# Moving the values' transfers from GpSimd to SP, lending more tiles and re-ordering a hybrid encoder layer's mixer

## The chip, the cores and the metric

The kernel runs on one core of one Trainium2 chip. The metric is device time in microseconds (us): the median of several runs of one launch. One of the executions was taken by the hardware profiler; its page and its trace are what this text reads. The engines are TensorE (PE; its weight loads are listed as PEld), VectorE (DVE), ScalarE (ACT), GpSimd (POOL) and SyncE (SP), which only issues transfers.

## The reference

One layer of an encoder with 512 positions and width 1024, in float32:

```python
x = x + 0.5 * swiglu(rms_norm(x, ffn1_norm), ...)      # d_ff 2752
u = rms_norm(x, mix_norm) @ w_in                        # [fourier 512 | q 8x64 | k 2x64 | v 2x64]
f = real(fft2(fourier, over positions and 128 channels of a group)) ; f = f @ fnet_w[g] + fnet_b[g]
a = softmax(rope(norm(q)) rope(norm(k)).T / 8) v        # 4 query heads to each key head, no mask
x = x + concat([f, a]) @ w_out
x = x + 0.5 * swiglu(rms_norm(x, ffn2_norm), ...)
y = rms_norm(x, final_norm)
```

## The kernel before

Three stages follow one another: feed-forward layer 1, the mixer, feed-forward layer 2. Every float32 operand of a matmul is held as a high part and a rest (suffixes `h` and `l` in the names below), and a product is three matmuls: high by high, high by rest, rest by high (`product`, L176 to L178). So each operand costs a cast and a subtraction (`lows`, L135) on some engine. The change is to the mixer, and to one step at the start of layer 2.

The mixer is written as small operations with names, and the list `ORDER` says in which order they are put out. Every engine takes its own ones in that order and waits where an operand, a tile or a PSUM bank isn't there yet. Lists beside it say which engine takes some of them: `LOWS_POOL` names the rests that GpSimd subtracts instead of VectorE, `HI_DVE` the high parts that VectorE casts instead of ScalarE, `ADDS_DMA` the rotary adds done by an accumulating DMA from GpSimd instead of VectorE, `SUMS_ACT` the broadcasts of the softmax sums done by ScalarE instead of GpSimd.

The names: `wk`, `wq0` to `wq3`, `wv`, `f0` to `f3`, `fw`, `o0` to `o7`, `g0` are weights, with `.r` (load by SP, 512 KB each, `fw` half of it), `.h`, `.l`. `k.0` to `k.7`, `q0.0`, `v.0` and so on are the projections' steps on TensorE, three matmuls of 512 columns each. `.sq`, `.pq`, `.s0`, `.s1` make the heads' norms (square, sums on TensorE, scaling, power on GpSimd); `.sw`, `.sd`, `.rc`, `.rs`, `.ra` the rotary turn (the other half of the pairs by ScalarE, its swap by four transfers of SP, product with the cosine, with the sine, add); `kw`, `kp`, `km` the norm's factor on the keys; `k0.0` to `k1.3` the keys' four parts, of which `k1.1` and `k1.2` are transfers; `q0.ah`, `.al`, `.bh`, `.bl` the queries' parts.

For tile t of the queries (0 to 3), key head b and block c of the keys' positions the scores are `s`tbc: two matmuls on TensorE. Then `m` (scaling and minimum, VectorE), `e` (exponential, ScalarE), `x` (32 by 32 transposition of the probabilities, VectorE), `h` and `l`. `p0` to `p3` multiply the turned probabilities with the values: 128 matmuls each, that use the array in four pieces of 32 rows. `p0` reads the t = 0, 1 and b = 0 ones, `p1` t = 2, 3 and b = 0, `p2` t = 0, 1 and b = 1, `p3` the others; all four read the same tiles `its`, so that the next one's `h` and `l` wait for the one before. The values are needed with their 32-row blocks repeated: tile `vrep`, which `vr0.0` to `vr0.3` (key head 0) and later `vr1.0` to `vr1.3` (key head 1, not before `p1` has read the old ones) fill with four transfers of 64 KB each, in pieces of 512 bytes. The source of `vr0` lies in the tile that `l103` writes. `o00.c` to `o31.a` take `p`'s results out, `z` and `r` divide by the sums and split.

The Fourier branch is `f00` to `f13` (projection for the positions' transform, `.0` and `.1` are twelve matmuls of 256 columns each; `.u`, `.e`, `.h`, `.l` take it out), `map0` and `map1`, `d00` to `d31` (the positions' transform; eight matmuls for d00, d10, d20, d30, six for the others, `.h`, `.l`), and `c0` to `c3` (channels: `.c`, `.s` on TensorE, three matmuls each; `.q`, `.t`, `.h` on ScalarE, `.o`, `.l` on VectorE). At last `y0.0` to `y7.7` are the output projection's steps, with `.x` (residual), `.h`, `.l` (input of layer 2), `.q`, `.a` (square and its sum). Layer 2 opens with two blocks of eight steps; ahead of the second block's first step stands the `column` (sums of the squares over partitions, on TensorE), and ahead of a later one the `row`, that turns the norm's factors.

All of this shares few tiles: two of tag `g` and two of tag `u`, taken in turn, four for the turned probabilities (`sq` and `x`), eight PSUM banks.

## Time and profile before

| | us |
|---|---|
| runs, median of 3 (lowest, highest) | 830.36 (829.91, 830.60) |
| the profiled execution | 829.37 |
| its span, first to last instruction | 827.5 |
| granted clock of TensorE, mean | 0.999 |
| busy: TensorE, VectorE, ScalarE, GpSimd | 818.3, 598.7, 460.4, 131.4 |

Times in a trace count from the start of the span. In a row of a group stand the line of the kernel, the engine, the operation, what it writes and reads, how often, then its busy time in us and the mean of one in ns, and the engine's idle time before it with what ended that. The mixer takes TensorE from about 335 to 488 us.

### The profile page before, as it was taken

How to read it: one execution, taken by the hardware profiler on the slowest of the kernel's cores; microseconds unless marked ns; L12 is line 12 of the kernel's file. 1: busy time of each engine (PE TensorE's matmuls, PEld its weight loads, DVE VectorE, ACT ScalarE, POOL GpSimd, SP SyncE). 2: the span in 40 equal slices, each digit the busy share in tenths (PEclk: the TensorE clock that was granted, in tenths of full speed). 3: DMA queues.
4: the chain of work that ended last, by engine and by line, in shares of the span. 5: the costliest groups of instructions: out<-in, count | busy, mean ns of one | idle time of the engine just before them, and what ended most of it. 6: DMA issues, size and time to landing. Idle time of an engine off the chain costs nothing.

```text
span 827.5 us, 14438 instructions
## 1 busy us (share of the span) xinstructions
PE 818.3 (99%) x5734; PEld 742.0 (90%) x5734; DVE 598.7 (72%) x927; ACT 460.4 (56%) x799; POOL 131.4 (16%) x135
## 2 busy tenths in 40 slices
PE   9999999999999999999999999999999999999997
PEld 6888998899989998888988888899988998899986
DVE  7987884578646857589998778878646884578562
ACT  7764663356434645567897357546623763266452
POOL 0121000000000000248794301200000000000001
PEclk9999999999999999999999999999999999999999
DMA  7787774457374514327350335877464664456122
GB/s 255 190 192 203 185 205 135 115 170 216 92 197 116 159 39 134 128 76 154 123 103 29 102 100 130 223 189 208 119 191 96 197 185 148 122 162 178 45 81 102
DMA packets 51028, 119.85 MB, mean 145 GB/s; under 512 B 5776, under 2 KB 14608, under 8 KB 50832
## 3 DMA queue, kind: packets, MB, share of 16 engines
q1 hardware_dynamic: 38128, 92.57, 33.7%
q0 software_dynamic: 12560, 26.09, 18.5%
q8 instruction: 45, 0.74, 0.4%
q10 hardware_dynamic: 272, 0.26, 0.1%
q14 instruction: 23, 0.19, 0.1%
HBM read 111.83 MB, written 2.10 MB: 138 GB/s over the span
## 4 chain that ended last, share of the span: by engine, by line
PE 93%; DVE 4%; issue 1%; POOL 1%; ACT 0%; DMA 0%; POOLq 0%; SPq 0%; DVEq 0%; ACTq 0%
PE r L453 23%; PE q L453 12%; PE dn L178 9%; PE dn L176 9%; PE dn L177 9%; PE p L453 6%; PE mix L176 3%; PE mix L177 3%; PE mix L178 3%; PE gu L791 3%; PE gu L176 3%; PE gu L177 3%; PE gu L178 3%; PE mix L1286 2%; PE last L1491 1%
## 5 line engine op out<-in xcount | busy, mean ns | idle before, releaser
L453 PE MATMUL r<-rt,ring 128*128 128x256 f32 x1686 | 204.9, 276 | 0.0
L453 PEld LDWEIGHTS r<-rt,ring 128*128 128x128 f32 x1686 | 198.5, 188 | 0.9
L177 PE MATMUL dn<-at,ring 128*128 128x512 f32 x295 | 114.8, 389 | 0.0
L178 PE MATMUL dn<-at,ring 128*128 128x512 f32 x295 | 114.8, 389 | 0.0
L176 PE MATMUL dn<-at,ring 128*128 128x512 f32 x295 | 114.8, 389 | 0.0
L453 PE MATMUL q<-rt,ring 128*128 128x256 f32 x840 | 106.6, 276 | 0.0
L398 ACT CAST ring<-s 128x1024 fp32r<-128x1024 f32 x70 | 73.5, 1050 | 58.1 <-DVE s L418 51.3
L453 PEld LDWEIGHTS q<-rt,ring 128*128 128x128 f32 x840 | 100.4, 188 | 0.0
L605 DVE SCALAR_TENSOR_TENSOR gx<-dn,gx 128x512 f32<-128x512 f32 x61 | 42.1, 691 | 80.4 <-PE dn L178 80.4
L370 POOL DMA_DIRECT2D s<-in_wgu x35 | 30.0, 858 | 424.0 <-DMA s<-in_wgu 186.3
L135 DVE TENSOR_TENSOR ring<-s,ring 128x1024 fp32r<-128x1024 f32 x70 | 85.3, 1218 | 0.6 <-ACT ring L398 0.6
L168 ACT CAST ring<-raw_dn 128x768 fp32r<-128x768 f32 (+2 forms) x48 | 40.8, 853 | 75.5 <-PE dn L177 70.5
L178 PEld LDWEIGHTS dn<-at,ring 128*128 128x128 f32 x295 | 55.4, 188 | 11.5
L177 PEld LDWEIGHTS dn<-at,ring 128*128 128x128 f32 x295 | 55.4, 188 | 11.1
L176 PEld LDWEIGHTS dn<-at,ring 128*128 128x128 f32 x295 | 55.4, 188 | 11.0
L453 PE MATMUL p<-rt,ring 128*128 128x256 f32 x420 | 53.3, 276 | 0.0
L135 DVE TENSOR_TENSOR ring<-raw_dn,ring 128x768 fp32r<-128x768 f32 (+2 forms) x48 | 46.7, 977 | 7.1 <-ACT ring L168 7.0
L453 PEld LDWEIGHTS p<-rt,ring 128*128 128x128 f32 x420 | 50.2, 188 | 0.0
L135 DVE TENSOR_TENSOR ring<-raw_g,ring 128x1024 fp32r<-128x1024 f32 x36 | 43.8, 1216 | 0.0
L135 DVE TENSOR_TENSOR at<-u,at 128x512 fp32r<-128x512 f32 x35 | 24.2, 692 | 20.3 <-ACT at L508 20.2
L496 DVE TENSOR_TENSOR u<-g,u 128x512 f32<-128x512 f32 x35 | 24.0, 686 | 19.8 <-ACT u L493 19.8
L398 ACT CAST ring<-raw_g 128x1024 fp32r<-128x1024 f32 x35 | 36.8, 1051 | 0.0
(332 smaller groups left out, 1548.6 us busy)
## 6 DMA issues: line engine op xcount, KB each, us to landing
raw_g<-in_wgu SPq DMA_DIRECT2D x36, 512.0 KB, 4.0
s<-in_wgu SPq DMA_DIRECT2D x70, 256.0 KB, 4.2
s<-in_wgu POOLq DMA_DIRECT2D x35, 512.0 KB, 5.6
raw_dn<-in_wd SPq DMA_DIRECT2D x44, 384.0 KB, 3.8
raw_u<-in_wgu SPq DMA_DIRECT2D x35, 256.0 KB, 4.1
raw_gu<-in_wgu SPq DMA_DIRECT2D x11, 512.0 KB, 3.6
raw_o<-in_wo SPq DMA_DIRECT2D x8, 512.0 KB, 3.7
raw_dn<-in_wd SPq DMA_DIRECT2D x5, 448.0 KB, 5.3
```

The costliest lines, as they stand in the source:

```text
L135: (by or nc.vector).tensor_tensor(out=lo, in0=src, in1=asf(hi), op=ALU.subtract)
L168: nc.scalar.copy(hi[:, :n, :], raw[:, :n, :])
L176: nc.tensor.matmul(ps, whi, mhi, start=first, stop=False)
L177: nc.tensor.matmul(ps, whi, mlo, start=False, stop=False)
L178: nc.tensor.matmul(ps, wlo, mhi, start=False, stop=last)
L370: nc.gpsimd.dma_start(out=blocks(t), in_=up, accum_op=ALU.add)
L398: nc.scalar.copy(ts[0], src)
L453: nc.tensor.matmul(ps[:, c], a[:, ks], b[:, i, c], start=first and i == 0 and o == 0, stop=i == KH - 1 and o == 2, skip_group_check=not fi ...
L496: nc.vector.tensor_tensor(out=self["u"], in0=self["g"], in1=self["u"], op=ALU.mult)
L605: nc.vector.scalar_tensor_tensor(out=x[d][:, t], in0=ps[:, t], scalar=0.5, in1=x[d][:, t], op0=ALU.mult, op1=ALU.add)
L791: nc.tensor.matmul(pss[c], w[:, k % 2, c], m[k], start=k == 0 and m is hh and w is hi, stop=k == KD - 1 and w is lo,)
L1286: nc.tensor.matmul(sets[st][a][:, : 8 * 32], vrep[rows, j], its[rows, o, :, 32 * j : 32 * j + 32], start=j == 0 and o == 0, stop=j == 15 a ...
```

## The change

The transfers `vr0`, `vr1`, `k1.1` and `k1.2` are issued by SP instead of GpSimd, on the same bytes seen as float32. The tags `g` and `u` get a third tile each (the norms' row tiles, which are idle during the mixer), in three kinds of places: swapped halves, values and Fourier parts share the `g` tiles, rotary products and `p`'s results the `u` tiles; the turned probabilities get a fifth tile. A tile is no longer taken in turn, but borrowed, and given back once the operations named have been put out. Thirteen names come into `LOWS_POOL` and eight leave it, `k` takes the place of `q2` in `ADDS_DMA`, z2 leaves `SUMS_ACT`, `HI_DVE` changes three names for five, `ORDER` is a new list of the same operations, and the row stands ahead of step 7 instead of 6.

```diff
 LOWS_POOL = """
-000 002 010 011 012 013 100 101 103 110 111 113 200 201 202 203 212 213 300 301 302 303 310 311 313 f3 o0 o1 o2 o4
-o5 o6 wq3
+001 002 003 010 011 012 013 100 102 103 110 111 112 113 200 201 202 203 211 212 213 300 301 302 303 312 313 f0 f1 f2
+f3 fw g0 o0 o1 o2 o7 wq2
 """.split()
 ADDS_DMA = """
-q2
+k
 """.split()
 SUMS_ACT = """
-z0 z1 z2 z3
+z0 z1 z3
 """.split()
 LOWS_DMA = """
...
 HI_DVE = """
-300 f0 o3 o4 wq3
+110 203 o3 o4 o6 o7 wq1
 """.split()
...
 ORDERED = {getattr(mybir.EngineType, e) for e in ("PE", "DVE", "Activation", "Pool", "SP")}
 ORDER = """
-wk.r wq0.r wv.r cos wk.h wk.l wq0.h k.0 k.1 k.2 k.3 k.4 wv.h k.5 wq0.l k.6 wq1.r k.7 k.sq q0.0 wq1.h n1.c k.pq q0.1
-wq3.r n1.m wq1.l wq2.r k.sw k.rs n1.p q0.2 q0.3 q0.4 q1.0 q0.5 k.s0 q1.1 wv.l q0.6 k.s1 k.rc q0.7 kw q0.rc k.ra
-wq2.h q1.2 v.0 q0.sw kp v.1 km q1.3 wq2.l q1.4 f0.r q0.sq q0.rs k1.0 q1.5 k0.0 q1.6 q0.ra k0.3 q0.pq q1.7 q0.ah k0.1
-v.2 v.3 q0.s0 q0.al v.4 k0.2 q0.bh q1.sq q0.bl s002 v.5 q0.s1 q1.sw s000 s001 m000 q1.rc q1.pq m002 q2.0 v.6 q1.sd
-v.7 q1.s0 k1.3 q1.rs q2.1 vt k1.1 s003 wq3.h vp e002 q2.2 q1.ra wq3.l m003 e000 x000 vm q1.ah q2.3 q1.al h000 q2.4
-q2.5 f0.h v0.h f1.r q2.6 x002 q2.7 q2.sw q1.s1 q3.0 s103 v0.l f1.h v1.h vr0.0 s102 k1.2 vr0.1 q3.1 m001 l000 q3.2
-m103 q3.3 f0.l q2.rc q2.sq e001 q1.bh q3.4 q3.5 m102 v1.l q3.6 e102 q1.bl f2.r s101 q2.sd e003 x102 x001 f3.r q3.7
-q3.sw q3.sd x003 s100 f2.h q2.rs q3.sq h002 f03.0 vr0.2 h001 e103 f1.l q3.rc m100 f01.0 h003 q2.ra m101 l001 q3.pq
-l003 q3.rs e100 q3.s0 f02.0 h102 q2.ah l002 q2.pq vr0.3 x100 q2.al q2.s0 q2.bh q3.ra f02.1 l102 q2.s1 f00.0 f00.1
-fw.r s203 s202 f2.l q3.s1 q3.ah x103 q3.al f03.1 s200 e101 f3.h f00.u m202 s201 h100 x101 s302 q3.bh z0.r f01.1 m203
-h103 f02.e e202 m200 h101 f3.l m201 e203 s300 x202 m300 f01.u e200 l100 f02.h l103 o1.r e201 z0.w fw.h f03.e x203
-o2.r q3.bl l101 f03.h f11.0 f02.l s303 f11.1 e300 f11.u m302 x200 p0 x300 e302 h200 f03.l s301 pos fw.l h300 f10.0
-q2.bl s112 h202 h203 f10.1 m301 o00.c m303 l202 x302 e303 m112 e301 l203 l200 o01.c x201 f10.u h302 o00.a f12.0
-o01.a s113 x301 f12.1 l300 h201 f13.0 x303 m113 e112 s110 h303 l302 f12.e x112 s013 h301 s011 s012 l201 f13.1 l303
-m110 m012 l301 m011 o2.h e113 e110 map1 f13.e m013 e012 x012 x110 map0 o2.l map1.h x113 map1.l o1.h o1.l f12.h f13.h
-map0.h e011 z1.r map0.l p1 f12.l z0.p f13.l e013 d00 o10.c o11.c r0.m d01 h112 vr1.1 o5.r d01.h s111 o10.a d00.h d11
-h012 o11.a vr1.2 l112 d10 d00.l d11.h d01.l l012 x013 m111 z1.w h110 c0.s d11.l s213 h113 l110 c0.c c0.q h013 m213
-e111 c0.t z1.p l013 d10.h d21 r1.m x111 d10.l l113 s010 d21.h m010 e213 d20 d31 c1.s h111 d21.l c1.c e010 d20.h c1.t
-c0.o c0.h d31.h l111 x010 d20.l x011 s212 h010 o0.r d30 m212 c1.q c0.l s313 c1.o c2.s h011 e212 s312 d30.h r1.h
-d31.l m312 vr1.0 vr1.3 m313 y2.0 c1.h c2.c c2.q x212 s311 c2.t d30.l e312 e313 c2.o l011 c3.s l010 x213 c3.c c1.l
-c3.q m311 s310 o0.h c3.t p2 x312 r0.h y2.1 e311 s210 c2.h c3.o c3.h m310 e310 y1.0 r0.l h212 y1.1 h312 c2.l s211
-z2.r c3.l x313 m210 o0.l o20.c h213 l212 l312 h313 l213 x311 m211 x310 e210 y2.2 h311 y1.2 y0.0 y0.1 e211 o20.a x211
-l313 h310 y0.2 x210 o21.c z2.w o21.a h210 l210 h211 y0.3 y2.3 l211 l311 r1.l y0.4 z3.r z2.p l310 o3.r z3.w y1.3 r2.m
-p3 y1.4 z3.p r2.h o30.c o31.c y1.5 r2.l y2.4 y2.5 y1.6 o30.a y0.5 o31.a r3.m y2.6 r3.h r3.l y2.7 o3.h y1.7 o5.h y0.6
-o3.l y0.7 o4.r y0.x y3.0 o5.l y3.1 y0.h y3.2 o4.h y1.x y3.3 o6.r y3.4 y0.q o4.l g0.r y3.5 y3.6 y5.0 y5.1 y0.l y4.0
-y3.7 y1.q y4.1 y4.2 y5.2 y5.3 y4.3 y2.x o7.r y5.4 o6.h y1.h y5.5 y3.x o6.l y6.0 y4.4 y3.q y4.5 y4.6 y3.a y2.h y5.6
-y6.1 y6.2 y5.7 y3.h y4.7 y1.a y2.l y5.x y3.l o7.h y6.3 y6.4 y6.5 o7.l y6.6 y7.0 y6.7 y7.1 y2.q y4.x y2.a y1.l y7.2
-y6.x y4.q y4.a g0.h y6.h y4.h y7.3 y7.4 y5.q y5.h g0.l y4.l y7.5 y7.6 y6.q y7.7 y5.a y6.l y6.a y7.x y5.l y7.h y7.q
-y7.l y7.a
+wk.r wq0.r wv.r cos wk.h wk.l wq0.h k.0 k.1 k.2 k.3 k.4 wv.h k.5 wq0.l k.6 wq1.r k.7 k.sq q0.0 wq1.h n1.c wq2.r
+wq1.l n1.m q0.1 k.pq f1.r k.sw q0.2 n1.p q0.3 k.rc q1.0 q0.4 q0.5 q0.6 q0.7 q1.1 k.s0 k.rs k.ra k.s1 q1.2 q1.3 q0.rc
+kw wv.l wq2.h q1.4 q1.5 v.0 kp q0.sw q0.rs v.1 q1.6 q1.7 v.2 km q1.sw k0.0 v.3 q0.sq q0.ra wq2.l v.4 k0.3 v.5 k0.1
+v.6 q0.ah k1.0 q0.bh q0.al k1.3 wq3.r q0.pq v.7 q1.sd q1.rc k0.2 q0.s0 q1.rs vt f0.r q0.s1 q2.0 s003 q1.ra q1.sq
+s000 wq3.h q0.bl m000 q2.1 wq3.l q1.ah s002 f0.h e000 q2.2 s001 m001 q2.3 f0.l x000 vp q2.4 q2.5 vm q2.6 h000 l000
+v0.h f2.r m002 k1.1 f3.r q2.7 e001 q2.sw q3.0 q1.pq q3.1 e002 f1.h q3.2 q2.rc q2.sq q1.al m003 q3.3 x001 q2.sd q3.4
+q3.5 q3.6 q1.s0 f1.l q3.7 q1.s1 q3.sw f2.h s102 e003 x002 v0.l v1.h q2.pq s100 q2.rs q2.ra f2.l s103 q3.rc q2.s0
+f01.0 m100 m102 k1.2 q3.sq q3.sd q2.s1 f01.1 q2.ah x003 s101 e102 e100 q2.al h001 h003 v1.l q3.pq q2.bh f03.0 vr0.0
+q3.rs s202 f01.u s203 h002 m103 vr0.3 q3.s0 s200 x100 m101 q3.ra x102 e101 h102 f03.1 m203 l001 x101 q3.s1 h100 l003
+s013 l100 q3.ah f02.0 m013 e103 l002 m200 h101 m202 x103 e203 f00.0 fw.r l101 vr0.2 f00.1 e013 q2.bl q3.al f3.h pos
+e202 f02.1 f03.e vr0.1 h103 s302 l102 l103 f00.u x203 f3.l s303 f11.0 m303 e200 f02.e x202 m302 f03.h x200 q3.bh
+e303 p0 x303 f03.l x013 q1.bh e302 h202 s301 q3.bl o00.c h303 h203 z0.r s201 h200 o01.c m301 e301 fw.h q1.bl f10.0
+o00.a l200 f10.1 m201 e201 f11.1 o01.a s110 l203 s010 s012 l303 x302 z0.w h302 o2.r x201 m010 l302 m110 f11.u m012
+s113 e010 s300 f12.0 f13.0 s011 o1.r x301 f10.u h201 m300 m113 l202 e110 e300 x300 h301 l201 o2.h m011 f13.1 z0.p
+fw.l e113 z1.r l301 x010 s112 h300 f13.e z1.w l300 x113 e012 r0.m map1 x110 e011 f12.1 f12.e x012 m112 map0 f02.h p1
+map1.h map0.h f02.l o2.l o1.h map0.l f12.h e112 f13.h map1.l s111 f12.l vr1.2 f13.l o10.c h110 m111 vr1.0 h013 d00
+o11.c o10.a e111 h113 d11 h012 d01 s312 o11.a l110 x111 d01.h l013 h010 m312 l113 z1.p d01.l x011 d00.h vr1.1 l012
+l010 e312 d00.l d31 r1.m d11.h d10 x112 d10.h s313 h111 d20 m313 c0.c d11.l d10.l l111 x312 c0.s d30 z2.r s213 h112
+d20.h vr1.3 c1.c c0.q c0.t h011 e313 d21 c1.s d21.h c0.o m213 d30.h c1.t o0.r d20.l d21.l d30.l s212 l112 m212 c1.q
+c1.o d31.h e213 l011 o1.l d31.l e212 c2.s s211 c2.c z2.w o0.h c2.q c2.t s311 p2 x212 m211 r0.h c3.s m311 c1.h o5.r
+e211 c0.h c2.o c2.h x313 c3.c o0.l x211 c0.l e311 s310 h313 l313 s210 c1.l c2.l h312 c3.q c3.t y1.0 h212 y1.1 l312
+y1.2 m310 c3.o e310 y2.0 x213 o20.c y2.1 x311 y0.0 l212 c3.h m210 o21.c x310 h211 e210 c3.l y2.2 y2.3 z2.p l211 o3.r
+y0.1 y0.2 z3.r o20.a x210 y1.3 h310 h213 h210 h311 o21.a l310 l213 r1.h l210 l311 r0.l z3.w r2.m y0.3 r2.h p3 r2.l
+y1.4 r1.l z3.p y1.5 o30.c y1.6 y2.4 o30.a o31.c o31.a r3.m y0.4 r3.h r3.l y2.5 y0.5 y2.6 y2.7 o3.h y1.7 y0.6 o3.l
+o4.r y0.7 o5.h y1.x y2.x y3.0 y3.1 y3.2 o6.r y3.3 y1.q o4.h y3.4 o4.l o5.l y3.5 y4.0 y5.0 y5.1 y0.x y3.6 y3.7 o6.h
+y4.1 y4.2 y0.q o6.l y3.x y5.2 y5.3 y5.4 y2.q y5.5 o7.r y1.a y5.6 y6.0 y5.7 y2.h y1.h y4.3 y1.l y4.4 y6.1 y6.2 y0.h
+y2.a y4.5 y4.6 o7.h y6.3 y4.7 o7.l y6.4 y5.x y3.q y6.5 y7.0 y2.l y3.a y3.h y7.1 g0.r y4.x y6.6 y7.2 y5.h y6.7 y4.h
+y3.l g0.h y7.3 y7.4 y5.l y6.x y5.q y7.5 y5.a y6.h y4.q g0.l y6.q y7.6 y7.7 y0.l y6.l y6.a y7.x y7.h y4.l y7.q y7.l
+y4.a y7.a
 """
...
             @op(f"{name}.sw")
             def _():
-                swaps[name] = sw = tp.tile([P, S], F32, tag="g", name=f"sw_{name}")
+                swaps[name] = sw = borrow(lent_g, f"{name}.ra")
                 if by_dma:
...
             @op(f"{name}.rc")
             def _():
-                rots[name] = r = tp.tile([P, S], F32, tag="u", name=f"rot_{name}")
+                users = ("k0.0", "k0.1", "k0.2", "k0.3", "k1.0", "k1.3") if name == "k" else (f"{name}.al", f"{name}.bl")
+                rots[name] = r = borrow(lent_u, *users)
                 if by_dma:
...
                 if v:
-                    op("k1.1")(lambda own=own, oth=oth, h1=h1, h2=h2: nc.gpsimd.dma_start(out=h1[oth], in_=h2[own]))
-                    op("k1.2")(lambda own=own, oth=oth, h1=h1, h2=h2: nc.gpsimd.dma_start(out=h2[oth], in_=h1[own]))
+                    op("k1.1")(lambda own=own, oth=oth, h1=h1, h2=h2: nc.sync.dma_start(out=asf(h1[oth]), in_=asf(h2[own])))
+                    op("k1.2")(lambda own=own, oth=oth, h1=h1, h2=h2: nc.sync.dma_start(out=asf(h2[oth]), in_=asf(h1[own])))
                     op("k1.3")(lambda own=own, h1=h1, h2=h2: lows(h2[own], rots["k"][own], h1[own]))
...
         @op("vt")
         def _():
-            rots["v"] = tp.tile([P, S], F32, tag="g", name="vt")
+            rots["v"] = borrow(lent_g, "vp")
             nc.scalar.copy(rots["v"], banks["v"])
...
             def spread(a):
...
                     src, dst = slice(32 * i, 32 * i + 32), slice(32 * a, 32 * a + 32)
-                    nc.gpsimd.dma_start(
-                        out=vrep[dst].rearrange("p (c i) e -> p c i e", i=4)[:, :, i],
-                        in_=stage[v][src].rearrange("p c o e -> p c (o e)"),
+                    nc.sync.dma_start(
+                        out=asf(vrep[dst].rearrange("p (c i) e -> p c i e", i=4)[:, :, i]),
+                        in_=asf(stage[v][src].rearrange("p c o e -> p c (o e)")),
                     )
...
             @op(f"f{h}{c}.e")
             def _():
-                fes[h, c] = e = tp.tile([P, 2, 256], F32, tag="g", name=f"fe{h}{c}")
+                fes[h, c] = e = borrow(lent_g, f"f{h}{c}.l").rearrange("p (a b) -> p a b", a=2)
                 for o, how in ((0, ALU.add), (1, ALU.subtract)):
...
             @op(f"c{g}.t")
             def _():
-                fos[g, 1] = o = tp.tile([P, S], F32, tag="g", name=f"fo{g}")
+                fos[g, 1] = o = borrow(lent_g, f"c{g}.l")
                 nc.scalar.activation(
...
             @op(f"x{n}")
             def _():
-                pool, how = (tp, {"tag": "sq"}) if len(turned) % 2 else (mt, {"tag": "x", "bufs": 2})
-                turned[n] = pool.tile([P, S], F32, name=f"x{n}", **how)
+                turned[n] = borrow(lent_x, f"h{n}", f"l{n}")
                 nc.vector.transpose(turned[n], probs[n])
...
             def copied(t):
                 if st not in pair:
-                    pair[st] = tp.tile([P, S], F32, tag="u", name=f"oo{st}")
+                    pair[st] = borrow(lent_u, f"r{st}.l")
                 for a in range(4):
...
         zall = [mp.tile([P, 4, 2], F32, name=f"za{t}") for t in range(4)]
+        def blanks(pool, tag, n):
+            return [pool.tile([P, S], F32, tag=tag, bufs=n, name=f"{tag}{i}") for i in range(n)]
+
+        lent_g = [*blanks(tp, "g", 2), n1.rb]
+        lent_u = [*blanks(tp, "u", 2), n2.rb]
+        lent_x = [*blanks(tp, "sq", 2), *blanks(mt, "x", 2), tp.tile([P, S], F32, tag="acc", name="acc_x")]
+        loans = []
+
+        def borrow(pool, *users):
+            t = pool.pop(0)
+            loans.append((set(users), pool, t))
+            return t
+
         scale = HD**-0.5
...
                 ops.pop(name)()
+                for users, pool, t in loans:
+                    users.discard(name)
+                    if not users:
+                        pool.append(t)
+                loans[:] = [loan for loan in loans if loan[0]]
         assert not ops, list(ops)
...
             prepare(2 * NF)
-        return [[gate(0, {}), gate(1, {0: column, 6: row})]]
+        return [[gate(0, {}), gate(1, {0: column, 7: row})]]
```

## The prediction

> **What bounds the kernel now.** I read the page first, then the busy time in stretches of 20 us through the mixer, then TensorE's waits and its timeline at the places they name.
>
> ```profile
> PE 818.3 (99%) x5734; PEld 742.0 (90%) x5734; DVE 598.7 (72%) x927; ACT 460.4 (56%) x799; POOL 131.4 (16%) x135
> PE 93%; DVE 4%; issue 1%; POOL 1%; ACT 0%; DMA 0%; POOLq 0%; SPq 0%; DVEq 0%; ACTq 0%
> ```
>
> TensorE is busy 818.3 of 827.5 us, and 93% of the chain that ended last is its own. The change leaves every matmul in place, so it can only win what TensorE idles, and it can lose without such a limit. The stretches show where the mixer is tight (columns: TensorE, weight loads, VectorE, ScalarE, GpSimd, clock, DMA share, GB/s):
>
> ```profile
> 360.00:380.00 20.00, 20.00 (x111) 17.26 (x109) 17.68 (x34) 13.67 (x28) 13.13 (x17) 1.00 0.73 157
> 380.00:400.00 20.00, 19.26 (x233) 18.21 (x237) 19.84 (x42) 14.83 (x34) 16.21 (x16) 1.00 0.58 147
> 400.00:420.00 20.00, 20.00 (x261) 18.45 (x254) 19.74 (x50) 17.59 (x49) 17.36 (x15) 1.00 0.33 99
> 420.00:440.00 20.00, 18.43 (x223) 16.07 (x222) 19.95 (x51) 18.78 (x49) 17.52 (x20) 1.00 0.41 68
> ```
>
> From 380 to 440 VectorE is busy 59.5 of 60 us. It has no slack left exactly where TensorE idles, and the granted clock is 1.00, so no clock explains it. TensorE's waits in the mixer name VectorE both times:
>
> ```profile
> PE mix L177 <- DVE ring L135: 1.4, 1, 1.4
> PE mix L1246 <- DVE fe L1135: 0.7, 1, 0.7
> ```
>
> A matmul's busy time covers the next one's issue, so a wait is read better from start to start. The timeline of TensorE at the three places:
>
> ```profile
> 391.55 0.28 PE L1115 MATMUL mix<-ring 128*128 128x256 f32 x1
> 391.66 0.28 PE L1116 MATMUL mix<-ring 128*128 128x256 f32 x1
> 392.68 0.50 PE L1246 MATMUL mix<-ks,qa 128*128 128x512 f32 x1 [0.74 <-DVE fe L1135]
> ...
> 430.16 0.40 PE L1247 MATMUL mix<-ks,qb 128*128 128x512 f32 x1
> 430.39 0.39 PE L176 MATMUL mix<-eh,more 128*128 128x512 f32 x1
> 430.92 0.50 PE L177 MATMUL mix<-el,more 128*128 128x512 f32 x1
> 431.26 0.39 PE L178 MATMUL mix<-eh,more 128*128 128x512 f32 x1
> 431.70 0.39 PE L176 MATMUL mix<-ring 128*128 128x258 f32 x1
> ...
> 432.63 0.28 PE L176 MATMUL mix<-ring 128*128 128x256 f32 x1
> 434.30 0.39 PE L177 MATMUL mix<-ring 128*128 128x256 f32 x1 [1.39 <-DVE ring L135]
> 434.53 0.28 PE L178 MATMUL mix<-ring 128*128 128x256 f32 x1
> ...
> 435.56 0.39 PE L1286 MATMUL mix<-its,vrep 32*128 32x256 f32 x4
> ```
>
> An undisturbed step is 0.11 us for 256 columns (391.55 to 391.66) and 0.23 for 512 (430.16 to 430.39). The step to 392.68 took 1.02, 0.91 too long (s300 waits for the bank that f02.e frees). Those to 430.92, 431.26 and 431.70 took 0.53, 0.34 and 0.44: 0.62 too long. Those to 434.30 and 434.53 took 1.67 and 0.23: 1.68 too long (c3.c waits for d30.l). Together **3.2 us**: that is the prize.
>
> **The change, part by part.**
>
> *VectorE's load.* What VectorE gives to GpSimd or does earlier is priced by these groups (six of VectorE and GpSimd, then two of ScalarE and one of VectorE that the parts below use):
>
> ```profile
> L135 DVE TENSOR_TENSOR ring<-raw_f,ring 128x1024 fp32r<-128x1024 f32 x2 | 2.4, 1219 | 0.0
> L135 DVE TENSOR_TENSOR its<-x,its 128x512 fp32r<-128x512 f32 x7 | 5.4, 797 | 0.1
> L878 DVE CAST more<-raw_wq 128x1024 fp32r<-128x1024 f32 x1 | 0.8, 779 | 0.0
> L956 DVE TENSOR_TENSOR rot_q<-rot_q,sw_q 128x512 f32<-128x512 f32 x3 | 2.0, 682 | 0.0
> L135 POOL TENSOR_TENSOR its<-x,its 128x512 fp32r<-128x512 f32 x25 | 32.8, 1339 | 5.9 <-ACT its L1272 5.9
> L135 POOL TENSOR_TENSOR ring<-raw_o,ring 128x1024 fp32r<-128x1024 f32 x4 | 9.7, 2419 | 16.3 <-ACT ring L878 15.6 <-DVE ring L878 0.8
> L920 ACT ACTIVATE early<-mix,qkg 128x512 f32<-128x512 f32 x3 | 2.1, 690 | 0.7 <-PE mix L178 0.6
> L1186 ACT CAST ring<-mix 128x255 fp32r<-128x255 f32 x4 | 1.5, 386 | 0.1
> L135 DVE TENSOR_TENSOR ring<-mix,ring 128x255 fp32r<-128x255 f32 x4 | 1.7, 416 | 0.0
> ```
>
> I count what the two lists put on VectorE from the first score's minimum (m000) to the last operation that p3 needs (l211 before, l311 after). Off: the rests of f0, f1, f2 (3 x 1.22 = 3.7) and of fw (half of one, 0.6), f0's high part (0.8), q1's rc, rs, ra and k1.3, now ahead of m000, and r0.l, now behind (5 x 0.68 = 3.4), six rests of turned probabilities (6 x 0.68 = 4.1, by the add of the same shape, since the group's mean of 0.80 may hold waits), h300 (0.4, half a cast), wq3's high part (0.8). On: wq3's rest (1.2), q2's add (0.7), four other rests (2.7), h110 and h203 (0.8). Net 13.8 - 5.4 = 8.4 less. Between s000 and p3 TensorE's list loses three projection steps and one of y, four times 3 x 0.23: 2.8 us less cover. So VectorE gains about **5 us of lead** by p3. It was late by 1.7 at c3.c; 5 us is enough to clear all three waits. I take the whole 3.2 us. From below: if the new list makes VectorE idle that long on ScalarE or GpSimd, nothing.
>
> *GpSimd.* It loses 34 issues and takes two more turned rests (2 x 1.34), 2.5 more weight rests (2.5 x 2.42 = 6.0) and the copy of z2 (1.3, by the rest of the same shape). What this risks is in one place: p2 needs eight rests on GpSimd that can't start before p1 has read the same tiles: 8 x 1.34 + 0.4 for h110 = 11.1 us.
>
> *SP in place of GpSimd.* Nearest rows: SP's own transfers of the same size inside SBUF, and the old ones:
>
> ```profile
> L934 SPq DMA_DIRECT2D sw_q<-early x12: 507/589/597, 358.6 to 378.8; - x12
> DMA to landing us min/median/max: 1.9/2.2/3.7
> 358.55 2.48 SPq L934 DMA_DIRECT2D sw_q<-early  x4
> L1075 POOL DMA_DIRECT2D vrep<-vst x16: 542/549/584, 417.7 to 432.1; - x16
> DMA to landing us min/median/max: 1.9/3.3/6.0
> rot_q<-sw_q POOLq DMA_DIRECT2D x1, 256.0 KB, 3.7
> ...
> 414.05 4.05 PE mix L1286 x119
> ```
>
> SP issues four in 2.48, 0.62 each, against 0.55 on GpSimd; they land in 2.2 against 3.3. So GpSimd is rid of 34 x 0.55 = 18.7, and SP gets about 21, of which it has plenty. The sixteen vr1 wait for p1's last read, in one row on SP: 15 x 0.62 + 2.2 = 11.5 us. The new list has between p1 and p2 fourteen score matmuls (14 x 0.23), 74 of 256 columns (d and c, 0.12 each) and z1.p (0.5): 3.2 + 8.9 + 0.5 = **12.6 us**. Before, the chain shows p1 from 414.05 to 418.10, and p2 at 435.56: 17.5 us. The cover has shrunk by 5 us; 1.1 is left, and 1.5 behind GpSimd's eight rests. The same ahead of p0: from q3's last matmul to p0 the new list has about 17.7 us of matmuls; the chain is q3's own pass (0.7), its four transfers (2.5), fw's load (0.3), the vr0 (15 x 0.62 + 2.2 = 11.5) and l103 (1.3), which overwrites their source: 16.3. Margin 1.4. I price both at nothing, and at 0.62 they hold. What queues behind on SP are loads of o weights, used tens of us later.
>
> The Trainium skill (DMA: Bandwidth & Descriptors, Rules for kernel authors) speaks against a gain here: spreading transfers over issuing engines doesn't speed them up, it only saves issue time. By that rule the move alone is worth 0, and the sum is the order's; the two sets of landings above are from different moments and don't decide it.
>
> *k's add by DMA.* It lands 3.7 us after issue instead of 0.68 on VectorE, but k's weights row needs the power on GpSimd and a transpose as well, and the first score moves from behind 22 steps of q and v to behind 25: 0 to 0.3, taken as 0.
>
> *Third and fifth tiles.* They only take waits away. 0.
>
> *New waits of the new list.* c2.s needs d21.l; between them on TensorE stand c1.s and s212, 3 x 0.12 + 2 x 0.23 = 0.8, against 0.39 + 0.42 on ScalarE and VectorE, with d20.l queued ahead of it (0.42): 0 to 0.5, I take 0.3. And the end:
>
> ```profile
> 493.22 0.68 DVE L1366 TENSOR_TENSOR acc<-acc,sq 128x512 f32<-128x512 f32 x1
> 494.15 0.95 PE L235 MATMUL ss<-ones,acc 128*128 128x2 f32 x8
> ...
> 464.51 2.39 POOL L135 TENSOR_TENSOR ring<-raw_o,ring 128x1024 fp32r<-128x1024 f32 x1 [0.78 <-DVE ring L878]
> 464.81 2.65 DVE L207 SCALAR_TENSOR_TENSOR ring<-gx,ring 128x512 fp32r<-128x512 f32 x1
> ```
>
> The last square is added at 493.90, 0.25 ahead of the column that reads it. The new list has one more add (y4.a, 0.68) behind y7.x: 0.4 late. The row at step 7 instead of 6 comes 3 x 0.23 = 0.7 later for what reads it; nothing on TensorE reads it before two more blocks of eight steps: 0 to 0.7, taken as 0. Places that I can't see: 0 to 2, taken as 0.3 (one wait the size of the small ones at 430).
>
> *Sum:* -3.2 + 0.3 + 0.4 + 0.3 = -2.2. The profiled execution took 829.37 (span 827.5 and 1.9 around it), so 827.2; the median of the runs is 830.36, 1.0 higher, so **828.2**.
>
> **Rivals.** *(a) VectorE's lead is spent* on waits for ScalarE, GpSimd and banks, and c and p3 are late as before: for it, the new list has 5 us less between p1 and p2, and ScalarE was busy 18.8 of 20 there; against it, the load counted above. Gain 0.5: 829.9. A single place can do it too: the last two rows show VectorE's operation of two SBUF inputs, started at 464.81, ending just behind GpSimd's of 464.51 (2.65 us, where the add of 493.22, of the same size, took 0.68). g0's rest now runs on GpSimd at the end: if it starts with y7.5, its 2.42 and then y5.a and y0.l (1.4) stand against three steps (2.1) and one matmul: 1.5 late, 829.7. The Trainium skill (SBUF - State Buffer, Who interferes with whom) has this as a lock that the second one waits for whole; the trace agrees.
>
> *(b) SP is slower at pieces of 512 bytes* than at the 2 KB rows of sw_q. From 0.70 us each p2 waits, from 0.71 p0. At 0.86: 2.5 at p2 and 2.2 at p0, 4.7 - 2.2 = +2.5: **832.9**. For it: no row shows SP with such pieces, and its issues lengthen when back to back; against it: GpSimd's cadence isn't hurt by them.
>
> *(c) The change doesn't do what it says:* if SP waits at q3's transfers or at a load and hands out the vr late, GpSimd's freed 18.7 us come too late to carry the added rests, and the lists run as before with p0 late by what SP lost; one load's landing (3.7 by the longest row above) less the margin of 1.4 gives 2.3, so 830.5, within 0.2%; its chance is in (a).
>
> **The numbers.** Forecast (faster by over 0.2%) 0.45; (a) with (c) 0.27, within 0.2%; (b) and other late transfers 0.28, slower. 0.2%, or 1.7 us, is about what a measurement of this kernel tells from nothing. The range goes from 827.0 (all 3.2, nothing new) to 832.9; the forecast's own is 827.0 to 828.7.
>
> **What would show it.** Right: no wait for VectorE at c3.c; the vr on SP at 0.6 us; p2 without a wait. Wrong: TensorE waiting at p0 or p2 for a DMA or GpSimd; VectorE again busy over 19.8 of 20 through 440 with c late.

## The result, and the profile after

| | before | after |
|---|---|---|
| runs, median of 8 each (lowest, highest), us | 829.67 (828.87, 830.60) | 833.00 (831.91, 835.70) |
| ratio, with its 95% interval | | 1.0039 (1.0029 to 1.0048) |
| the profiled execution, us | 829.37 | 831.91 |
| its span, us | 827.5 | 830.1 |

The kernel after is slower by 0.39%, 3.3 us. The forecast was 828.2 and faster, with a range up to 832.9; the sign is wrong and the median lies just outside. The profiled execution is the fastest of its eight, and their spread has grown from 1.7 to 3.8 us; both come up again below.

The page's busy line, its chain, and the stretches of 20 us from 360 on (columns as in the prediction):

```profile
PE 820.1 (99%) x5734; PEld 742.9 (89%) x5734; DVE 596.3 (72%) x924; ACT 457.2 (55%) x796; POOL 119.7 (14%) x107
PE 92%; DVE 3%; ACT 2%; issue 1%; POOL 1%; DMA 1%; SPq 1%; POOLq 0%; DVEq 0%; ACTq 0%
```

```profile
360.00:380.00 20.00, 20.00 (x111) 17.21 (x112) 17.47 (x34) 14.74 (x28) 11.57 (x6) 1.00 0.44 123
380.00:400.00 20.00, 18.27 (x220) 17.18 (x222) 19.15 (x38) 14.79 (x33) 15.24 (x12) 1.00 0.56 166
400.00:420.00 20.00, 20.00 (x248) 18.61 (x244) 19.11 (x49) 18.29 (x45) 13.80 (x10) 1.00 0.10 28
420.00:440.00 20.00, 20.00 (x257) 17.98 (x253) 19.57 (x52) 17.45 (x50) 15.43 (x11) 1.00 0.49 139
```

VectorE did get lighter (57.8 of 60 us from 380 to 440, against 59.5), GpSimd too, and the hole that TensorE had in 420 to 440 is closed (20.00 against 18.43). A new one stands in 380 to 400: 18.27 against 19.26. The clock is 1.00 throughout, so it explains nothing. In the chain, ScalarE has come up from 0 to 2%, DMA and SP's queue from 0 to 1% each. TensorE's waits name four new places:

```profile
PE mix L1286 <- POOL its L135: 0.9, 1, 0.9
PE mix L1247 <- DVE qa L135: 0.8, 1, 0.8
PE mix L176 <- ACT fq L1213: 0.6, 1, 0.6
PE ss L235 <- DVE acc L1366: 0.4, 1, 0.4
```

Read from start to start in TensorE's timeline they are longer:

```profile
391.90 0.28 PE L1117 MATMUL mix<-ring 128*128 128x256 f32 x1
392.97 0.47 PE L1247 MATMUL mix<-ks,qa 128*128 128x512 f32 x1 [0.79 <-DVE qa L135]
...
395.43 0.39 PE L1286 MATMUL mix<-its,vrep 32*128 32x256 f32 x4
396.76 0.52 PE L1286 MATMUL mix<-its,vrep 32*128 32x256 f32 x8 [0.94 <-POOL its L135]
...
433.62 0.40 PE L1248 MATMUL mix<-ks,qb 128*128 128x512 f32 x1
434.00 4.50 PE L1286 MATMUL mix<-its,vrep 32*128 32x256 f32 x128
...
440.04 0.40 PE L1248 MATMUL mix<-ks,qb 128*128 128x512 f32 x1
441.00 0.50 PE L176 MATMUL mix<-eh,ring 128*128 128x512 f32 x1 [0.57 <-ACT fq L1213]
...
495.51 0.39 PE L178 MATMUL gu<-ring 128*128 128x512 f32 x1
496.33 0.91 PE L235 MATMUL ss<-ones,acc 128*128 128x2 f32 x7 [0.43 <-DVE acc L1366]
```

s302 (392.97) is 0.96 late. Inside p0, four matmuls start at 395.43 and the next at 396.76: 1.2 late. The column (496.33) came 0.82 after the matmul ahead of it, where 0.23 is undisturbed: 0.59 late. y1.0 (441.00) waited 0.74 for its bank, behind the score matmul at 440.04, and p3 0.4 inside itself. p2 (434.00) is late by 0.16 only. The three old waits, c3.c's 1.68 among them, are gone. So 3.2 us of old waits went, and 4.1 us of new ones came, 2.2 of them within 4 us around 394.

The spans of the two profiled executions differ by 2.63 us, and stretch by stretch this is 0.57 ahead of the mixer's first matmul, 1.02 in the mixer, 0.66 from y7.7 to the last matmul (the column and what follows it) and 0.38 from the last matmul to the end. The last piece comes with the move to SP: from the start of the last matmul to the end of the span it is 6.14 or 6.15 us in the profiles of this document where GpSimd issues the transfers (before, tiles_only, vr_pool) and 6.52 to 6.54 in the other eleven. There SP waits at the end for the signals of its transfers, one after another, and in after six of these waits, 0.06 us each, come behind the landing of the last store, where in before they came ahead of it.

### The profile page after: what moved, and what is told of

Read it like the earlier page. It is cut to its first block, busy times and chain, and to the rows that moved or that the text cites. A ratio compares the mean times of both kernels' runs of the same rounds, so it can differ in the third digit from the quotient of the medians.

```text
span 830.1 us, 14432 instructions
## 1 busy us (share of the span) xinstructions
PE 820.1 (99%) x5734; PEld 742.9 (89%) x5734; DVE 596.3 (72%) x924; ACT 457.2 (55%) x796; POOL 119.7 (14%) x107
## 4 chain that ended last, share of the span: by engine, by line
PE 92%; DVE 3%; ACT 2%; issue 1%; POOL 1%; DMA 1%; SPq 1%; POOLq 0%; DVEq 0%; ACTq 0%
PE r L453 23%; PE q L453 11%; PE dn L178 9%; PE dn L177 9%; PE dn L176 9%; PE p L453 6%; PE mix L176 3%; PE mix L178 3%; PE mix L177 3%; PE gu L791 3%; PE gu L176 2%; PE gu L177 2%; PE gu L178 2%; PE mix L1286 1%; PE last L1509 1%
## 5 line engine op out<-in xcount | busy, mean ns | idle before, releaser
L135 DVE TENSOR_TENSOR ring<-s,ring 128x1024 fp32r<-128x1024 f32 x70 | 85.3, 1219 | 0.6 <-ACT ring L398 0.6
L135 DVE TENSOR_TENSOR ring<-raw_dn,ring 128x768 fp32r<-128x768 f32 (+2 forms) x48 | 46.8, 978 | 7.1 <-ACT ring L168 6.9
L135 DVE TENSOR_TENSOR ring<-raw_g,ring 128x1024 fp32r<-128x1024 f32 x35 | 42.6, 1217 | 0.0
L135 DVE TENSOR_TENSOR at<-u,at 128x512 fp32r<-128x512 f32 x35 | 24.2, 693 | 20.2 <-ACT at L508 20.2
```

What stands on the lines that cost most here:

```text
L135: (by or nc.vector).tensor_tensor(out=lo, in0=src, in1=asf(hi), op=ALU.subtract)
```

## The experiments

Twelve kernels, in three sets on three chips, each set beside the kernel before, so that the ratios are what compares them. The mixer's length here is read off TensorE's timeline of one profile, from the first matmul of k.0 to the first one of y7.7; that of tiles_only is 0.5 us longer than before's at an equal median, so a difference of that size says little:

| kernel | median, us | ratio to before | 95% interval | mixer, us |
|---|---|---|---|---|
| before | 829.7 to 830.0 | | | 152.5 |
| after, second time | 832.50 | 1.0037 | 1.0023 to 1.0051 | 153.6 (first time 153.5) |
| pos_split | 830.98 | 1.0011 | 1.0003 to 1.0020 | 152.6 |
| pos_late | 829.72 | 0.9996 | 0.9987 to 1.0005 | 150.8 |
| lows_back | 831.13 | 1.0012 | 1.0004 to 1.0021 | 152.5 |
| y4a_early | 832.06 | 1.0028 | 1.0017 to 1.0039 | 153.7 |
| best1 | 829.74 | 0.9998 | 0.9989 to 1.0007 | 152.1 |
| best2 | 829.76 | 1.0000 | 0.9992 to 1.0009 | 151.6 |
| best3 | 828.80 | 0.9984 | 0.9976 to 0.9993 | 150.4 |
| tiles_only | 829.88 | 0.9998 | 0.9990 to 1.0007 | 153.0 |
| sp_only | 839.56 | 1.0106 | 1.0091 to 1.0121 | 163.2 |
| sp_fixed | 831.09 | 1.0015 | 1.0007 to 1.0024 | 153.5 |
| vr_pool | 851.17 | 1.0250 | 1.0231 to 1.0270 | 172.6 |

**The transfers of `pos`.** In the trace of after GpSimd stood idle for 3.85 us ahead of l103, which overwrites the source of vr0, and p0 waited for l103. The row puts this down to an exponential of ScalarE on which l103 doesn't depend; the last vr0 landed at 395.08, 0.34 us ahead of l103's start and 5.9 us after its issue. Just ahead of that GpSimd issues `pos`. The theory: those bytes hold up the last vr0.

> The kernel after, with one name moved in ORDER: pos (three transfers, 1.4 MB, issued by GpSimd for the Fourier branch) stands behind s301, past p0, as in the kernel before, not ahead of vr0.1. Theory T (the last vr0 transfers land late because they share the DMA engines with pos): the trace of after has the two last vr0 transfers landing 3.7 and 5.9 us after issue, l103 on GpSimd behind them and 1.2 us of TensorE waiting in p0; s302 waits 0.96 on VectorE, whose subtraction and rest beside it took 1.21 and 1.68 instead of 0.69. Expected: landings back to 2 to 2.5 us, p0 without a wait (-1.2), s302's wait shorter by 0 to 0.9: 0.9985 to 0.9975 of after. Rival R1 (the landing is SP's own, from its 16 issues in a row): landings stay, nothing gained, 1.000. Rival R2 (the wait only moves, since the next operation is late too): p0's wait falls and another of the same size comes within 30 us, 1.000.

```diff
-... q2.bl q3.al f3.h pos e202 f02.1 f03.e vr0.1 h103 s302 l102 l103 ...
+... q2.bl q3.al f3.h e202 f02.1 f03.e vr0.1 h103 s302 l102 l103 ...
-... e302 h202 s301 q3.bl o00.c ...
+... e302 h202 s301 pos q3.bl o00.c ...
```

One name moved takes the ratio from 1.0039 to 0.9996: the whole loss. The expected 1.2 to 2.1 us were too few. The trace says where they come from. VectorE's and GpSimd's rows in after, then in pos_late (start, duration, engine and operation, idle time ahead in brackets):

```profile
388.32 0.65 POOL L1437 DMA_DIRECT2D late<-in_chan  x1
388.96 0.56 POOL L1437 DMA_DIRECT2D late<-in_pos  x1
389.21 1.21 DVE L135 TENSOR_TENSOR its<-sq,its 128x512 fp32r<-128x512 f32 x1
389.49 0.56 POOL L1437 DMA_DIRECT2D late<-in_odd  x1
390.05 1.52 POOL L135 TENSOR_TENSOR its<-sq,its 128x512 fp32r<-128x512 f32 x1
390.44 1.68 DVE L135 TENSOR_TENSOR qb<-u,qb 64x512 fp32r<-64x512 f32 x1
392.13 0.68 DVE L135 TENSOR_TENSOR qa<-u,qa 64x512 fp32r<-64x512 f32 x1
...
395.42 1.29 POOL L135 TENSOR_TENSOR its<-x,its 128x512 fp32r<-128x512 f32 x1 [3.85 <-ACT e L1262]
```

```profile
388.34 1.29 POOL L135 TENSOR_TENSOR its<-sq,its 128x512 fp32r<-128x512 f32 x1
388.88 1.30 DVE L135 TENSOR_TENSOR its<-sq,its 128x512 fp32r<-128x512 f32 x1
...
390.20 0.69 DVE L135 TENSOR_TENSOR qb<-u,qb 64x512 fp32r<-64x512 f32 x1
390.90 0.68 DVE L135 TENSOR_TENSOR qa<-u,qa 64x512 fp32r<-64x512 f32 x1
```

There are two effects. First, with the three issues in front of it, GpSimd's l102 runs at 390.05 instead of 388.34. VectorE's rest of q2 (qb) starts beside it and takes 1.68 us instead of 0.69: it ends 0.55 after l102 does (392.12 and 391.57). In pos_late VectorE's l101 is caught by l102 in the same way (1.30, ending 0.55 after it) but the two rests of q behind it are free. q3's part (qa), for which s302 waits, starts 1.23 us earlier (0.33 of that is a lead that this execution had by q3.7 already), and s302's 0.96 is gone. The Trainium skill (SBUF — State Buffer, Who interferes with whom) describes this as a lock between VectorE's operations of two SBUF inputs and GpSimd's reads of SBUF; these ends agree with it. Why l101 took 1.21 in after (1.23 in after_2, 1.38 in pos_split), though GpSimd did nothing but issue in its first 0.8 us, isn't settled.

Second, the landings. SP's issues of vr0 and vr1, and the time from issue to landing over both, in after, then pos_late:

```profile
L1076 SPq DMA_DIRECT2D vrep<-its x16: 592/599/668, 378.8 to 389.1; - x16
...
DMA to landing us min/median/max: 2.0/2.0/5.9
```

```profile
L1076 SPq DMA_DIRECT2D vrep<-its x16: 599/599/670, 378.6 to 388.9; - x16
...
DMA to landing us min/median/max: 2.0/2.0/2.8
```

SP is as fast in both and the issues stand at the same times, but the longest landing is 5.9 us beside `pos` and 2.8 without it. (The 512 KB load that SP issues right behind the last vr0 stands there in pos_late as well, so it isn't the cause by itself.) The times of landing point at `pos` too: in after the last two vr0 transfers were issued 0.18 and 0.19 us behind the first two transfers of `pos`, of 256 KB and 1 MB, and landed 0.31 and 0.39 us behind them, at 392.18 and 395.08. And every profile of these kernels agrees: the longest landing of a vr0 is 5.9, 6.1 and 6.4 us in the three with `pos` ahead of it (after twice, y4a_early), 2.7 to 2.9 in the five with `pos` moved (pos_late, lows_back, best1 to best3). To part the two effects:

> The kernel after, with most of one transfer taken out of its place: at pos, ahead of vr0.1, GpSimd still issues three transfers (chan 256 KB, the first 128 KB of pos, odd), and the other 0.9 MB of pos go out by a fourth one behind s301. It asks what of the 3.3 us that moving pos won is the bytes in flight and what is GpSimd's time and VectorE's waiting beside it. Theory T1 (bytes: the last vr0 transfers land late beside 1 MB): they land within 2.5 us, p0's 1.2 us go, and s302's 0.96 stays, since GpSimd's three issues still stand there: -1.2 us, about 0.9985 of after (832.0 by today's runs of it, 831.8). Theory T2 (GpSimd's issues and rests in VectorE's way push the whole chain): s302 and p0 keep their waits, 1.000 of after. Theory T3 (both waits hang on the bytes): as pos_late, 829.7.

```diff
 for n, k in (("chan", 4 * P), ("pos", 4 * 514), ("odd", 258)):
-    nc.gpsimd.dma_start(out=late[n], in_=A[n])
+    # of pos only the first 257 columns here; the rest by a new step pos2, behind s301
```

```profile
PE mix L1247 <- DVE qa L135: 0.9, 1, 0.9
PE mix L176 <- ACT fq L1213: 0.6, 1, 0.6
PE ss L235 <- DVE acc L1366: 0.4, 1, 0.4
```

TensorE's waits in pos_split have lost p0's and kept s302's: T1. The longest landing is 3.8, again just behind the transfer of `pos` ahead of it (393.24 and 393.03). The ratios put the bytes at 2.2 to 2.3 us (1.0037 and 1.0039 to 1.0011) and GpSimd's place at 1.2 (1.0011 to 0.9996), with intervals of some 0.8 us either way about each ratio; the mixer's length says 0.9 to 1.1 and 1.7, 0.4 of the latter at y1.0. The sum is firm, its parting less so.

> The kernel after as it is, run again with the others, since moving pos won 3.3 us by the medians where the profiled execution (its fastest, 831.91) shows waits of 2.2 us at s302 and p0. Theory T (the wait in p0 hangs on a landing that differs from run to run): median 833, spread of 3 us again, and a profiled execution slower than 831.9 waits longer than 1.2 us in p0. Rival: the waits at s302 and p0 are as in the first profile and the difference lies elsewhere in the span.

The second profile of after, of an execution of 832.51, has a longest landing of 6.1 and 1.33 us of waiting in p0, and s302's 0.98. There the trace names the transfers as what GpSimd waited for (engine, tile and line that waited for L1076, us in total, times):

```profile
  POOL its L135: 4.0, 1
```

So it is the same picture, a little longer, as T says; no execution near 835 was profiled, so what the slowest ones wait for isn't seen. That `pos` is behind the spread fits the runs (832.1 to 835.8 here, 830.7 to 832.6 in pos_split, 828.6 to 830.2 in pos_late), but it isn't shown: a single execution of eight (835.70, the others up to 833.59) and of six (835.78, the others up to 832.95) makes most of the spread of after.

**SP, and the order, each alone.**

> The kernel before, its order, tiles and lists, with vr0, vr1, k1.1 and k1.2 issued by SP. Theory T (the move alone is worth about nothing, since GpSimd isn't what TensorE waits for in before, and costs nothing where nothing large shares the DMA engines): 0.999 to 1.001 of before. Rival R (SP is the harm): p0 or p2 late by 1 to 4 us, 1.002 to 1.005 of before.

```diff
 (the kernel before)
-nc.gpsimd.dma_start(out=vrep[dst]..., in_=stage[v][src]...)      # and k1.1, k1.2
+nc.sync.dma_start(out=asf(vrep[dst]...), in_=asf(stage[v][src]...))
```

```profile
372.10 3.36 SPq L1075 DMA_DIRECT2D vrep<-its  x4
375.50 0.60 SPq L1032 DMA_DIRECT2D ks<-ks  x1
376.15 2.53 SPq L1075 DMA_DIRECT2D vrep<-its  x4
...
379.41 2.46 SPq L934 DMA_DIRECT2D sw_q<-early  x4
...
386.25 1.87 PE L966 MATMUL mix<-halves,early 128*128 128x2 f32 x8 [6.54 <-ACT early L912]
```

The loss is 8.8 us by the ratio (9.7 by the medians), far beyond what either theory gave, and by neither's way: SP takes its list in order, vr0.0, k1.2 and vr0.1 wait for their sources, and the swaps of q2 and q3 (sw_q) come behind them. q2's swap goes out at 379.41, right behind a load of 512 KB, and its four transfers land 2.7 to 3.9 us after their issue; ScalarE stands behind the swapped half, and the sums of q3 (L966) wait 6.5 us.

> The kernel before with the transfers issued by SP as in sp_only, and vr0.0, k1.2 and vr0.1 moved in ORDER behind q3.sd, so that on SP they no longer stand ahead of the swaps of q2 and q3. In sp_only TensorE waited 6.5 us for q2's swap, which SP issued at 379.4 behind vr0.0, k1.2 and vr0.1, and the granted clock was 0.66 in the 20 us after. Theory T (what cost 9.7 us is the order of SP's queue, and the move itself is worth nothing): no wait at q3.pq, 0.999 to 1.001 of before. Rival R1 (SP's transfers cost something of their own): 1.002 to 1.005. Rival R2 (GpSimd free of 34 issues lets VectorE's three waits shrink): 0.996 to 0.998.

```diff
-... v1.h vr0.0 s102 k1.2 vr0.1 q3.1 ... q3.sw q3.sd x003 ...
+... v1.h s102 q3.1 ... q3.sw q3.sd vr0.0 k1.2 vr0.1 x003 ...
```

The 6.5 us are gone, and with them all but 1.2 us of the loss (1.0015): the place in SP's list it was. What is left shows as new waits at two score steps (0.3 and 0.6 in the timeline, put down to ScalarE's casts of turned probabilities); the three old waits are all there, c3.c's with 1.5 us in one step. So GpSimd's 18.7 us do nothing by themselves (R2 is out), and the move costs a little in the old order: 0.38 of the 1.2 us is the longer end behind the last matmul; for the rest, whether SP or its place in the list costs it isn't told apart.

> The kernel after, with vr0, vr1, k1.1 and k1.2 issued by GpSimd again; order, tiles and lists of after. Theory T (issuing on SP isn't what costs; the new list needs it): GpSimd has 34 issues of 0.55 more, 8.8 us of them between p1 and p2 beside eight rests of 1.34; p2 waits for one or the other 4 to 9 us, and p0 0 to 4: 1.005 to 1.015 of after. Rival R (transfers on SP are the harm: cadence 0.645 against 0.55, landing): 0.997 to 1.000 of after.

```profile
399.32 0.38 PE L1286 MATMUL mix<-its,vrep 32*128 32x256 f32 x1
405.08 0.80 PE L1286 MATMUL mix<-its,vrep 32*128 32x256 f32 x3 [5.38 <-DMA vrep<-its]
407.05 1.23 PE L1286 MATMUL mix<-its,vrep 32*128 32x256 f32 x16 [1.17 <-POOL its L135]
```

(The edit is the reverse of that in sp_only, made to the kernel after.) It costs 18 us on top of after: theory T's sign, more than its 4 to 12.5 us, and at another place. p0, not p2, pays most: 5.65 and 1.6 us for vr0 and l103 that GpSimd can't do in time, and s302 waits 3.5; behind these waits TensorE's clock was halved for a while (last section). The new order needs SP.

> The kernel before, its order, lists, row and GpSimd's transfers, with the third tiles for g and u and the fifth for turned probabilities, borrowed as in after. Theory T (in the old order no engine waits for these tiles): 0.999 to 1.001 of before. Rival R1 (the tiles alone shorten VectorE's waits): 0.996 to 0.998. Rival R2 (the kernels with lent tiles start the mixer 0.25 to 0.84 us later in the profiles so far; if the tiles' places in memory do that): 1.0005 to 1.001, with the first projection at 335.6 or later.

0.9998: the tiles alone are worth nothing in the old order, and R1 is out. With one of the third tiles or the fifth left out, the new order asks for a tile that hasn't been given back yet (counted in the list, it holds three, three and five at once, the old one two, two and four), so it needs them all the same. R2 isn't settled. This profile starts the mixer 1.06 us later than that of before, at an equal median, and the two profiles of after start it 0.57 and 1.06 later, so the opening, before any changed step, does differ between executions; nearly all of the difference arises in the first 8 us of the span. But the three profiles without lent tiles (before, sp_fixed, sp_only) start the mixer earliest of all fourteen, at 335.58 to 335.77 against 335.83 to 336.65, and the interval of tiles_only, 0.9990 to 1.0007, doesn't exclude the lower end of R2.

**VectorE's load.**

> pos_late (829.7 us) with the four rests of f0, f1, f2 and fw on VectorE again, 4.3 us of its work between 360 and 410, which GpSimd takes 2.42 each for. Theory T (the prediction's: VectorE's load up to p3 sets the waits, and GpSimd has room): TensorE waits for VectorE again, 1 to 4 us, 831 to 833.5. Rival (VectorE has slack left there, or GpSimd's relief gives as much back): 829.2 to 830.2.

```diff
 LOWS_POOL = """
-... 313 f0 f1 f2 f3 fw g0 o0 ...
+... 313 f3 g0 o0 ...
```

1.4 us more than pos_late, in T's range: s302 waits for VectorE again (`PE mix L1247 <- DVE qa L135: 1.1, 1, 1.1` in the list, 1.25 in the timeline), and small waits come at 423.3 and 431.8 (0.34 and 0.37). 4.3 us of VectorE's work in this stretch are worth 1.4 us of time.

**The end, and the o weights.**

> The kernel after, with one name moved in ORDER: y4.a (an add of 0.68 us on VectorE) stands ahead of y6.a, not behind y7.x. Theory T: the column of layer 2 waits 0.59 us in after because one add more stands behind the last y; without it the column waits 0 to 0.1, -0.5 us, 0.9994 of after. Rival R: g0's rest on GpSimd (484.6 to 487.0) holds VectorE there, the wait stays, 1.000.

```diff
-... y6.q y7.6 y7.7 y0.l y6.l y6.a y7.x y7.h y4.l y7.q y7.l y4.a y7.a
+... y6.q y7.6 y7.7 y0.l y6.l y4.a y6.a y7.x y7.h y4.l y7.q y7.l y7.a
```

The column is out of TensorE's list of waits, where p0, s302 and y1.0 still stand: T as to the wait. By the timeline 0.3 of its 0.6 come back as small steps just ahead of it, so the gain is 0.3; the median is 0.4 to 0.9 us below the two of after, which is within their intervals.

> The kernel after with pos behind s301 and y4.a ahead of y6.a together. Theory: both work apart, pos_late's 829.7 less the column's wait of 0.59: 829.1, 0.9990 of before. Rival: the add put earlier takes time of VectorE that y7 needs, 829.7.

> As best1, and c3.q, c3.t (ScalarE, they free the bank that y1.0 writes) ahead of s210, so that on ScalarE they run before the last of two casts (h312). Theory: y1.0's wait of 0.36 goes, 828.8, 0.9987 of before. Rival: h312 and its rest are late by 0.65 then and p3 waits that much more: 829.1 to 829.5.

best1 joins the edits of pos_late and y4a_early; best2 adds:

```diff
-... h313 l313 s210 c1.l c2.l h312 c3.q c3.t y1.0 ...
+... h313 l313 c3.q c3.t s210 c1.l c2.l h312 y1.0 ...
```

Both miss: 829.74 and 829.76, no better than pos_late. best1's profile is as fast as pos_late's up to p2, and from p2 to p3 1.4 us slower, though nothing there differs between the two kernels. The rows of ScalarE in best1 and in pos_late show where:

```profile
433.14 1.05 ACT L878 CAST ring<-raw_o 128x1024 fp32r<-128x1024 f32 x1 [1.60 <-DMA raw_o<-in_wo]
```

```profile
431.80 1.05 ACT L878 CAST ring<-raw_o 128x1024 fp32r<-128x1024 f32 x1 [0.26 <-DMA raw_o<-in_wo]
```

ScalarE stood 1.60 us for the load o0.r, and everything behind the cast with it, c3.q among it, which frees y1.0's bank. The load stands on SP behind the sixteen vr1, and in best1 the second of these took SP 1.84 us to issue, where the longest in pos_late took 0.62 (1.03 in after): o0.r went out 1.2 us later. Why one issue is long isn't known. In after the load stands at the same place:

```profile
420.14 10.84 SPq L1076 DMA_DIRECT2D vrep<-vst  x16
431.09 7.54 SPq L154 DMA_DIRECT2D raw_o<-in_wo  x4
```

```profile
434.75 1.05 ACT L878 CAST ring<-raw_o 128x1024 fp32r<-128x1024 f32 x1 [0.69 <-DMA raw_o<-in_wo]
...
440.56 0.39 ACT L1213 COPY fq<-mix 128x256 f32<-128x256 f32 x1
```

> As best1 (pos behind s301, y4.a ahead of y6.a), and o0.r, a load of 512 KB by SP, ahead of the vr1 transfers instead of behind them. In best1's profile ScalarE idled 1.60 us for that load (0.26 in pos_late, which was 1.1 us faster from p2 to p3), and TensorE waited 0.79 at s310, 0.73 at y1.0 and 0.39 in p3. Theory T (those waits hang on the load's landing behind sixteen transfers): ScalarE doesn't wait for it, the three waits shrink by 0.8 to 1.5 in all, 828.3 to 829.0. Rival (VectorE, busy 19.95 of 20 us there, keeps them): 829.4 to 829.9.

```diff
 (best1)
-... f12.l vr1.2 ... h010 o0.r ... / c1.t o0.r d20.l ...
+... f12.l o0.r vr1.2 ... / c1.t d20.l ...
```

ScalarE's cast, the stretch from 420 to 440, and TensorE's one wait in the mixer, in best3:

```profile
431.73 1.04 ACT L878 CAST ring<-raw_o 128x1024 fp32r<-128x1024 f32 x1
```

```profile
420.00:440.00 20.00, 20.00 (x231) 17.75 (x231) 19.89 (x54) 18.91 (x54) 17.83 (x13) 1.00 0.47 129
```

```profile
PE mix L1286 <- DVE its L135: 0.2, 1, 0.2
```

T: ScalarE doesn't idle for the load, though one vr1 issue was long here too (1.27), s310 and y1.0 wait no more, and what is left in the mixer are three steps of c2.s, together 0.3 too long, 0.17 ahead of p2 and one wait in p3 (0.2 in the list, 0.49 in the timeline). TensorE is busy 20.00 of 20 us in all four stretches from 360 to 440, with VectorE at 19.89 in the last. 828.80 us, 0.9984 (0.9976 to 0.9993): a little faster than both kernels. From best1 it is 0.9 us by the medians and 1.2 by the ratios, whose intervals overlap. That it lies 0.6 us from the figure forecast for the kernel after is no support for that sum, since it is another kernel.

## Why the prediction was wrong, step by step

- *The prize of 3.2 us* is right: the three waits are there in before, tiles_only and sp_fixed, and none of them stands in after. That *VectorE's load* sets such waits is borne out by lows_back, which brings 1.4 us back for half of the 8.4, though at s302 and not at c3.c; the new order and the new lists were not run apart, so which of them closed the three isn't shown. In best3 the mixer is 2.1 us shorter, where the prediction's terms for it give 2.6 (3.2 less 0.3 and 0.3); by the ratios best3 gains 1.3, since 0.4 is lost again by the column and 0.4 behind the last matmul, for which the prediction has no term.
- *SP's row of vr0 ahead of p0, priced at nothing with a margin of 1.4 us*: this is the step that failed, and it made the sign. The chain was worked with a landing of 2.2 us. The cadence was fine (0.645 for 0.62), the landing was not: 5.9 us for the last one, 3.7 more, which is 2.3 beyond the margin. The diff moves `pos`, 1.4 MB, from behind p0 to ahead of vr0.1, and the prediction doesn't mention it, neither its bytes nor GpSimd's three issues. pos_split and pos_late price it at 3.3 us together. The sign to look for was named, TensorE waiting at p0 for a DMA or GpSimd. With `pos` out of the way (pos_late) the kernel is level with before, not 2.2 us faster; what is still missing there is told under o0.r, the column and the end.
- *s302.* The same move put l102 beside two of VectorE's operations. The lock was in the prediction, as rival (a), but at the end, with g0's rest; it bit at 390 and cost 0.96 there.
- *"What queues behind on SP are loads of o weights, used tens of us later"* is wrong for the first of the four behind vr1: o0.r is used 3.7 us after its issue at the earliest (431.09 to 434.75), and ScalarE waited 0.3 to 1.6 us for it. best3 puts about 1 us on that, within intervals of 0.8 us either way.
- *The column*: 0.4 predicted, 0.59 measured. *The row at step 7*: nothing waits for it, as taken. *c2.s* (0.3): its three steps are 0.09, 0.12 and 0.10 too long in after, 0.3 as taken. *k's add by DMA*: no wait of TensorE ahead of s302, as taken (the steps ahead of the old first score are 21, not 22; nothing hangs on it). *p2's two margins* (1.1 and 1.5) held: in after the last vr1 landed at 432.40 and the eighth rest ended at 431.89, 1.6 and 2.1 us ahead of p2, which is 0.16 late.
- *Rival (b)*, SP slower from 0.70 us on, is out: vr0 took 592 to 670 ns of issue each, 0.645 from one to the next, and in vr1's row only one issue was longer (1.03 in after, 1.84 at most in the profiles looked at). The 0.86 us, from which the top of the range is worked, stood in no row. *Rival (c)* has the right victim, p0 behind a late vr0, and the wrong cause: SP handed the transfers out on time, and they came late. It was given no chance of its own and priced at 2.3; the bytes cost about that.
- *Rule on issuing engines* (the Trainium skill, DMA: Bandwidth & Descriptors, Rules for kernel authors: transfers of all issuing engines share the same 16 DMA engines): the traces agree, in the direction that the prediction didn't draw from it. A transfer put on another queue than `pos` wasn't out of its way (5.9 us to its landing, 2.8 at most without `pos`).
- The size of the loss by medians, 3.3 us, is more than the 2.5 of the profiled executions; the opening is 0.57 of these 2.5, and whether that belongs to the lent tiles or to the execution isn't settled (tiles_only).

## What to carry to other kernels

When an order is rewritten, list every transfer that changed its neighbours, with its bytes, and not only those that the change is about: what is short and urgent must not share the DMA engines with what is long and not. A chain with a margin of 1.4 us can't be priced at nothing if one landing in it can be 3 us longer, and the trace of before showed that it can (6.0 stood in the rows of vrep itself). And an engine that issues in order hands on one wait to all that stands behind it: before moving transfers to a queue, ask for each one behind them when its first reader comes.
